# The last up tile and the first two down products in a written engine order, with the down loads issued in written order

## The chip, the cores and the metric

The kernel runs on one core of a Trainium2 chip. The metric is the device time of one execution in microseconds (us). A core has engines that each work through their own list of instructions in order and wait for one another through semaphores: TensorE for matrix products (PE in the profile, PEld its weight loads), VectorE (DVE), ScalarE (ACT), GpSimd (POOL) and SyncE (SP), which here only issues the transfers between device memory and the on-chip buffers.

## The reference

One layer of a streaming encoder on a sequence of 1024 frames with 1024 channels. A token mixer with three attention branches comes first; the change lies behind it, in the channel mixer, whose code is

```python
def _conv_ffn(h, w_up, conv_w, conv_b, w_down):
    a, g = jnp.split(h @ w_up, 2, axis=-1)
    a = lax.conv_general_dilated(a, conv_w[:, None, :], window_strides=(1,),
                                 padding=[(CONV_W - 1, 0)],
                                 dimension_numbers=('NWC', 'WIO', 'NWC'),
                                 feature_group_count=D_FF) + conv_b
    return (jax.nn.gelu(a) * g) @ w_down
...
        h = _rmsnorm(x, norm_g[l, 2]) * (1.0 + sc2) + sh2
        y = _conv_ffn(h, w_up[l], conv_w[l], conv_b[l], w_down[l])
        x = x + g2 * _rmsnorm(y, norm_g[l, 3])
```

`w_up` has 1024 x 5632 elements, `w_down` 2816 x 1024, and the convolution is causal, over three frames, per channel.

## The kernel before

All matrices are float32. Each operand is split into a high part, rounded to the reduced format that TensorE multiplies (ACT makes it, as a copy), and a low part, the difference (DVE makes it); a product is three matmuls: high by high, high by low, low by high. A block product is done by a scheme with seven products of half-size blocks in place of eight, so sums and differences of blocks are formed first on both sides.

**Up.** The 2816 hidden channels are 22 tiles of 128, numbered 0 to 21. `up_tile(f)` does the seven products of tile f (`product`, lines 1246 to 1248, 12 matmuls of 512 columns each). They accumulate in three PSUM banks X, Y and V: X takes the products B11, T2, T3 and T4, Y takes B21, V takes T1 and B22. Between two products on one bank something reads the intermediate sum: `p1` (ACT, line 1263) reads X after B11, `p5` (ACT, line 1269) reads V after T1, `u2` (ACT, line 1272) reads X after T2, and one half of `g` (DVE, line 1278) reads X after T3. The next product on that bank waits for that read. After the seventh product ACT reads the rest of `a` (line 1281). Then come the convolution (ACT line 1285, DVE lines 1286 and 1287), the GELU (ACT line 1288), the product with `g` (POOL line 1289) and `down_left`, which makes the left operands of the down projection from the tiles of a pair, splits them and writes them to device memory (lines 1306 to 1308, `L_spill`; the last two tiles go to `F_spill`). The tiles of those operands rotate over four buffers, so a split waits until the fourth transfer before it has left its buffer.

**Down.** Five chunks of four hidden tiles, and a rest of two. A chunk has seven products of 24 matmuls (lines 1627 to 1629), in `PLAN` order on two sets of four banks, XB and VB; after each, ACT copies or DVE adds the banks into `acc` (lines 1634 and 1632). The left operands are loaded from `L_spill` into `ring`, twelve slots in three buffers (line 1492); these three buffers are those that held the left operands S2, S4 and S3 of the up products, so the first four loads wait until tile 21 is done with S2. The right operands come from four rows of `w_down` per chunk: two tiles `wd` and, for the first chunk, two parts of `work` (line 1507), which takes the place of `big0`, the left operand of B11 and B21. `right_split` (lines 1501 and 1502) splits them, and `total` (line 1537) forms T1 to T4. Four pieces of a small product with `w_ada` (lines 185 to 210) are done beside it.

**Order.** Some stretches are written out by hand: within `tc.manual_schedule(engines=...)` the named engines take the program's order. Everything else is placed by a list scheduler with a timing model, each engine for itself; there the order of the code is only a preference. In the kernel before, tiles 1 to 21 and the whole down part are left to the scheduler, and so is the order of SP's transfers.

Names of a buffer carry a tile or chunk number and a serial number; both are dropped in the profile's names, so `X<-left_S,rT` stands for the products T2 and T3, `V<-left_S,rB` for B22 and `X<-big,rT` for T4.

Of the kernel before, what the change touches and what calls it, by code (L numbers as in the profile page):

```python
# [16 lines left out]
P = 128  # L17
# [4 lines left out]
HALF = 512  # L22
# [38 lines left out]
def encoder_layer(ctx: ExitStack, tc: tile.TileContext, x, w_ada, w_in, w_branch, w_out, w_up, w_down,  # L61
# [1188 lines left out]
    def up_tile(f, r, parts):  # L1250
# [36 lines left out]
        dve.scalar_tensor_tensor(cv[:, 2:], a[:, 0:S - 2], w0[:, f:f + 1], cv[:, 2:], op0=OP.mult, op1=OP.add)  # L1287
        act.activation(cv, cv, AF.Gelu_apprx_tanh)  # L1288
        pool.tensor_tensor(cv, cv, g, op=OP.mult)  # L1289
        down_left(f, cv)  # L1290
# [175 lines left out]
    for f in range(1, NF):  # L1466
        tile_ = up_tile(f, r, [(0, HALF)])
        go(tile_)
        for _ in before:
            pass  # L1470
        if f + 1 < NF:
            r, ws = up_weights(f + 1)
            for _ in ws:
                pass
        go(tile_, 5)
        before = tile_
    for _ in before:
        pass
# [5 lines left out]
    XB = [bank(t, f"X_{i}") for i, t in enumerate("ddss")]  # L1484
    VB = [bank(t, f"V_{i}") for i, t in enumerate("snnn")]
# [11 lines left out]
    def right_split(src, eng, name, alloc=None):  # L1497
        nonlocal n_right
        n_right += 1
        t = alloc(name, (P, 2, HALF)) if alloc else (f4 if n_right % 4 == 0 else k4)(name, F32R, (P, 2, HALF))  # L1500
        act.activation(t[:, 0], src, AF.Copy)  # L1501
        eng.tensor_tensor(t[:, 1], src, t[:, 0].bitcast(F32), op=OP.subtract)
        return t
# [9 lines left out]
    def chunk_load(c):  # L1513
        for k in range(2):
            loaded[c, k] = [w_load(4 * c + 2 * k, raw4),
                             w_load(4 * c + 2 * k + 1, e4 if c else (lambda n: work[:, 6 + k]))]
# [11 lines left out]
    def prepared(c):  # L1528

        src = [{}, {}]  # L1530
        for k in range(2):
            wa, wb = loaded[c, k]
# [67 lines left out]

    chunk_load(0)
    lefts = all_lefts()
    ahead = [next(lefts) for _ in range(L_AHEAD)]
    preps = all_prepared()
    ready = [next(preps) for _ in range(D_AHEAD)]
    G2 = [t2(f"G2_{g}") for g in range(2)]
    G2_AT = {0: (40,), 1: (42, 44), 2: (46,)}
    seen = set()
    for c in range(N_C):
        for n, (banks, starts, into) in enumerate(PLAN):  # L1610
            if n == D_LOAD:
                if c + 1 < N_C:
                    chunk_load(c + 1)
                else:
                    last_in = [w_load(4 * N_C + j, raw4) for j in range(2)]
            nxt_ = next(preps, None)
            if nxt_ is not None:
                ready.append(nxt_)
            nxt_ = next(lefts, None)
            if nxt_ is not None:  # L1620
                ahead.append(nxt_)
            ops = list(zip(ahead.pop(0), ready.pop(0)))
            for i in range(4):
                o = banks[i]
                for k, (l, r) in enumerate(ops):
                    lh, ll = (l[:, j, i * P:(i + 1) * P] for j in range(2))
                    pe.matmul(o, lh, r[:, 0], start=(starts and k == 0), stop=False, skip_group_check=True)  # L1627
                    pe.matmul(o, lh, r[:, 1], start=False, stop=False, skip_group_check=True)  # L1628
                    pe.matmul(o, ll, r[:, 0], start=False, stop=(k == 1), skip_group_check=True)  # L1629
                dst = C[into][i]  # L1630
                if (into, i) in seen:
                    dve.tensor_tensor(dst, dst, o, op=OP.add)  # L1632
                else:
                    act.activation(dst, o, AF.Copy)
                    seen.add((into, i))
# [62 lines left out]
```

## Time and profile before

| | us |
|---|---|
| median of three runs | 1599.38 |
| lowest and highest of them | 1599.19, 1602.44 |
| the profiled execution | 1600.86 |
| its span, first to last instruction | 1599.1 |
| PE busy | 1497.8 (94%) |
| DVE busy | 1187.5 (74%) |
| ACT busy | 786.4 (49%) |
| POOL busy | 561.5 (35%) |

The span is what the trace shows; the device time of that execution is 1.8 us longer. PE's mean granted clock over the span is 0.984 of full speed. The share of busy time is a mean over stages with different limits; the mixer ends and the up part begins at about 925 us, the down part at 1370 us, and the last matmul ends at 1587.2 us. Shares of DMA are of 16 transfer engines.

### The profile page before, as it was taken

The page shows a single profiled execution, that of the slowest core. Times are in us where ns is not written, and L with a number is a line of the kernel's source. Part 1 is how long each engine was busy: PE and PEld are TensorE (multiplying, and loading weights), DVE is VectorE, ACT ScalarE, POOL GpSimd, SP SyncE. Part 2 cuts the span into 40 slices and gives each one's busy share as a digit, 9 for nine tenths or more (in the row PEclk, how much of TensorE's full clock was granted, in tenths as well). Part 3 has the DMA queues.
Part 4 walks back from the last instruction along what each step waited for, and adds up shares of the span by engine and source line. Part 5 has one row for each costly group of instructions (what it writes and reads, how often), then busy time and mean ns, then how long its engine had stood idle before and what let it go on. Part 6 is the DMA issues. An engine that isn't in the chain of part 4 may idle for free.

```text
span 1599.1 us, 21251 instructions
## 1 busy us (share of the span) xinstructions
PE 1497.8 (94%) x7322; PEld 1239.6 (78%) x7322; DVE 1187.5 (74%) x2166; ACT 786.4 (49%) x1462; POOL 561.5 (35%) x408
## 2 busy tenths in 40 slices
PE   3989999989998999989999999999999999899997
PEld 2768888777886888767888787788888887788885
DVE  6765888999669854547536779888777777778768
ACT  4434598786554454542235455555555554522222
POOL 3441544433453543204542223222222221433205
PEclk9999999999998999999999999999999999999999
DMA  9541333423544332346676413544444445996742
GB/s 282 136 106 32 113 110 87 149 80 119 162 143 131 95 117 86 109 145 189 205 273 217 146 53 96 179 164 165 151 150 149 145 146 197 403 350 225 269 174 105
DMA packets 187871, 253.98 MB, mean 159 GB/s; under 512 B 14891, under 2 KB 145139, under 8 KB 187763
## 3 DMA queue, kind: packets, MB, share of 16 engines
q1 hardware_dynamic: 187763, 252.62, 47.4%
q8 instruction: 58, 0.95, 0.2%
q14 instruction: 50, 0.41, 0.1%
HBM read 169.75 MB, written 74.97 MB: 153 GB/s over the span
## 4 chain that ended last, share of the span: by engine, by line
PE 63%; DVE 19%; DMA 6%; ACT 5%; issue 4%; POOL 2%; SPq 1%; DVEq 0%; POOLq 0%; ACTq 0%
PE X L1246 4%; PE X L1247 4%; PE X L1248 4%; PE g L247 4%; PE g L248 4%; PE g L249 4%; DVE ada_acc L198 2%; PE X L1627 2%; PE X L1629 2%; PE X L1628 2%; PE V L1246 2%; PE V L1247 2%; PE V L1248 2%; DVE junk L649 2%; PE V L1629 2%
## 5 line engine op out<-in xcount | busy, mean ns | idle before, releaser
L647 ACT ACTIVATE junk<-sc,thr 128x512 bf16<-128x512 f32 (+2 forms) x93 | 80.2, 862 | 30.7 <-DVE thr L668 25.7
L649 DVE TENSOR_SCALAR_CACHE_REDUCE junk<-sc,thr 128x384 bf16<-128x384 f32 (+2 forms) x93 | 89.6, 964 | 1.8
L1212 POOL TENSOR_TENSOR T<-ua 128x512 f32<-128x512 f32 x21 | 27.2, 1296 | 174.9 <-DVE rT L1198 165.2
L198 DVE SCALAR_TENSOR_TENSOR ada_acc<-ada_raw,c_act,ada_acc 128x256 f32<-128x256 f32 x120 | 81.4, 725 | 1.3 <-DMA ada_raw<-in_w_ada 1.2
L1289 POOL TENSOR_TENSOR cv<-cv,g 128x1024 f32<-128x1024 f32 x22 | 57.6, 2617 | 45.9 <-ACT cv L1288 36.9
L1247 PE MATMUL X<-left_S,rT 128*128 128x512 f32 (+1 forms) x184 | 70.8, 385 | 0.2 <-DVE left_S L1092 0.2
L1246 PE MATMUL X<-left_S,rT 128*128 128x512 f32 (+1 forms) x184 | 70.8, 385 | 0.0
L1248 PE MATMUL X<-left_S,rT 128*128 128x512 f32 (+1 forms) x184 | 70.7, 384 | 0.0
L1632 DVE TENSOR_TENSOR acc<-acc,X 128x512 f32<-128x512 f32 x68 | 45.8, 683 | 16.8 <-PE X L1629 16.5
L1501 ACT ACTIVATE T<-work 128x512 fp32r<-128x512 f32 x40 | 25.2, 631 | 63.7 <-PE V L1629 26.9
L1213 POOL TENSOR_TENSOR ug<-ug 128x512 f32<-128x512 f32 x22 | 32.6, 1482 | 66.5 <-DVE ua L1206 66.5
L1001 POOL TENSOR_TENSOR M<-M,tgb 128x1024 f32<-128x1024 f32 x12 | 30.6, 2559 | 68.1 <-DVE tgb L999 68.1
L1632 DVE TENSOR_TENSOR acc<-acc,V 128x512 f32<-128x512 f32 x56 | 37.8, 683 | 19.2 <-PE V L1629 19.0
L1627 PE MATMUL X<-T,ring 128*128 128x512 f32 x120 | 47.3, 394 | 0.0
L1629 PE MATMUL X<-T,ring 128*128 128x512 f32 x120 | 47.1, 392 | 0.0
L1628 PE MATMUL X<-T,ring 128*128 128x512 f32 x120 | 46.9, 391 | 0.0
L1197 ACT ACTIVATE rT<-ua 128x512 fp32r<-128x512 f32 x45 | 28.2, 627 | 35.9 <-DVE ua L1210 22.9
L1198 DVE TENSOR_TENSOR rT<-ua,rT 128x512 fp32r<-128x512 f32 x45 | 38.9, 865 | 9.3 <-ACT rT L1197 8.8
L1198 DVE TENSOR_TENSOR rB<-ua,rB 128x512 fp32r<-128x512 f32 x44 | 41.2, 939 | 2.0 <-ACT rB L1197 0.9
L1246 PE MATMUL X<-big,rT 128*128 128x512 f32 (+1 forms) x92 | 36.4, 396 | 5.8 <-DVE g L1278 5.8
L1247 PEld LDWEIGHTS X<-left_S,rT 128*128 128x128 f32 x184 | 34.5, 188 | 7.9 <-DVE left_S L1092 0.4
L615 DVE SCALAR_TENSOR_TENSOR sc<-rl,wi,sc 128x512 f32<-128x512 f32 (+3 forms) x30 | 30.2, 1038 | 14.0 <-ACT rl L614 14.0
(982 smaller groups left out, 5563.0 us busy)
## 6 DMA issues: line engine op xcount, KB each, us to landing
ring<-L_spill SPq DMA_DIRECT2D x70, 512.0 KB, 6.1
L_spill<-S SPq DMA_DIRECT2D x40, 512.0 KB, 4.2
L_spill<-A SPq DMA_DIRECT2D x30, 512.0 KB, 3.3
raw_g<-in_w_in SPq DMA_DIRECT2D x24, 512.0 KB, 4.3
ada_raw<-in_w_ada SPq DMA_DIRECT2D x24, 512.0 KB, 3.8
ua<-in_w_up SPq DMA_DIRECT2D x22, 512.0 KB, 4.3
ug<-in_w_up SPq DMA_DIRECT2D x22, 512.0 KB, 3.9
gate_spill<-tg SPq DMA_DIRECT2D x20, 512.0 KB, 2.6
```

The costliest lines, as they stand in the source:

```text
L198: dve.scalar_tensor_tensor(acc[:, k % 2], per_k[k], c_act[:, k:k + 1], acc[:, k % 2], op0=OP.mult, op1=OP.add)
L247: pe.matmul(o, wh[:, k], hh[:, k, ts_], start=(k == 0), stop=False)
L647: act.activation(junk_a[:, 0:n], scores[b], AF.Sign, scale=-1.0, bias=t_f, accum_out=cnt[:, j:j + 1])
L649: dve.tensor_scalar(junk_d[:, 0:n], scores[b], t_f, None, op0=OP.is_lt, op1=OP.add, accum_out=cnt[:, j:j + 1])
L1198: eng.tensor_tensor(hl_[1], src, hl_[0].bitcast(F32), op=OP.subtract)
L1246: pe.matmul(oc, r[:, 0, k], lh, start=(first and k == 0), stop=False, skip_group_check=True)
L1247: pe.matmul(oc, r[:, 0, k], ll, start=False, stop=False, skip_group_check=True)
L1248: pe.matmul(oc, r[:, 1, k], lh, start=False, stop=(last and k == 3), skip_group_check=True)
L1627: pe.matmul(o, lh, r[:, 0], start=(starts and k == 0), stop=False, skip_group_check=True)
L1628: pe.matmul(o, lh, r[:, 1], start=False, stop=False, skip_group_check=True)
L1629: pe.matmul(o, ll, r[:, 0], start=False, stop=(k == 1), skip_group_check=True)
L1632: dve.tensor_tensor(dst, dst, o, op=OP.add)
```

## The change

The last up tile (21), what is left of tile 20, the preparation of the first right operands and the first two down products are put into one written order for ACT, DVE, POOL and PE. In that order tile 21's last product follows the whole first down product, the second down product follows it, and the adds of the first stand between them. The banks are given out anew (three of XB from the tag of Y, three of VB from that of V, one of each from that of X), the fourth split takes a buffer of the larger pool, and of the four pieces of the product with `w_ada` one moves from the first chunk to the second and one from the second to the third. SP's transfers of the down part, up to the fifth product of the last chunk, are issued in the order of the code, and a chunk's four weight loads come at two places of the chunk before it (three at product 2, one at product 4) in place of one.

```diff
@@ -1285,8 +1285,10 @@
         act.activation(cv, a, AF.Identity, bias=cb[:, f:f + 1], scale=w2[:, f:f + 1])
         dve.scalar_tensor_tensor(cv[:, 1:], a[:, 0:S - 1], w1[:, f:f + 1], cv[:, 1:], op0=OP.mult, op1=OP.add)
         dve.scalar_tensor_tensor(cv[:, 2:], a[:, 0:S - 2], w0[:, f:f + 1], cv[:, 2:], op0=OP.mult, op1=OP.add)
+        yield
         act.activation(cv, cv, AF.Gelu_apprx_tanh)
         pool.tensor_tensor(cv, cv, g, op=OP.mult)
+        yield
         down_left(f, cv)
 
 
@@ -1463,26 +1465,23 @@
             pass
 
     before = first
-    for f in range(1, NF):
+    for f in range(1, NF - 1):
         tile_ = up_tile(f, r, [(0, HALF)])
         go(tile_)
         for _ in before:
             pass
-        if f + 1 < NF:
-            r, ws = up_weights(f + 1)
-            for _ in ws:
-                pass
+        r, ws = up_weights(f + 1)
+        for _ in ws:
+            pass
         go(tile_, 5)
         before = tile_
-    for _ in before:
-        pass
 
 
     ring = [opp.tile([P, 4, 2, HALF], F32R, tag="left", name=f"ring{j}") for j in range(3)]
     work = hp.tile([P, NB, S], F32, tag="h", name="work")
     acc = hp.tile([P, NB, S], F32, tag="h", name="acc")
-    XB = [bank(t, f"X_{i}") for i, t in enumerate("ddss")]
-    VB = [bank(t, f"V_{i}") for i, t in enumerate("snnn")]
+    XB = [bank(t, f"X_{i}") for i, t in enumerate("sssd")]
+    VB = [bank(t, f"V_{i}") for i, t in enumerate("nnnd")]
     n_left = 0
 
     def left_load(src):
@@ -1497,7 +1496,7 @@
     def right_split(src, eng, name, alloc=None):
         nonlocal n_right
         n_right += 1
-        t = alloc(name, (P, 2, HALF)) if alloc else (f4 if n_right % 4 == 0 else k4)(name, F32R, (P, 2, HALF))
+        t = alloc(name, (P, 2, HALF)) if alloc else (f4 if n_right % 4 == 0 and n_right > 4 else k4)(name, F32R, (P, 2, HALF))
         act.activation(t[:, 0], src, AF.Copy)
         eng.tensor_tensor(t[:, 1], src, t[:, 0].bitcast(F32), op=OP.subtract)
         return t
@@ -1510,10 +1509,14 @@
     N_C = 5
     loaded = {}
 
-    def chunk_load(c):
-        for k in range(2):
-            loaded[c, k] = [w_load(4 * c + 2 * k, raw4),
-                             w_load(4 * c + 2 * k + 1, e4 if c else (lambda n: work[:, 6 + k]))]
+    def chunk_load(c, which=(0, 1, 2)):
+
+        for j in which:
+            if j == 1:
+                for k in range(2):
+                    loaded[c, 1, k] = w_load(4 * c + 2 * k + 1, e4 if c else (lambda n: work[:, 6 + k]))
+            else:
+                loaded[c, 0, j // 2] = w_load(4 * c + j, raw4)
 
...
+    def down_mm(n, ops):
+        banks, starts, _ = PLAN[n]
+        for i in range(4):
+            o = banks[i]
+            for k, (l, r) in enumerate(ops):
+                lh, ll = (l[:, j, i * P:(i + 1) * P] for j in range(2))
+                pe.matmul(o, lh, r[:, 0], start=(starts and k == 0), stop=False, skip_group_check=True)
+                pe.matmul(o, lh, r[:, 1], start=False, stop=False, skip_group_check=True)
+                pe.matmul(o, ll, r[:, 0], start=False, stop=(k == 1), skip_group_check=True)
+            yield
+
+    seen = set()
+
+    def down_add(n, i):
+        banks, _, into = PLAN[n]
+        dst = C[into][i]
+        if (into, i) in seen:
+            dve.tensor_tensor(dst, dst, banks[i], op=OP.add)
+        else:
+            act.activation(dst, banks[i], AF.Copy)
+            seen.add((into, i))
+
+    def next_ops():
+        nxt_ = next(lefts, None)
+        if nxt_ is not None:
+            ahead.append(nxt_)
+        return list(zip(ahead.pop(0), ready.pop(0)))
+
+    lefts = all_lefts()
+    preps = all_prepared()
+    G2 = [t2(f"G2_{g}") for g in range(2)]
+    G2_AT = {1: (40, 42), 2: (44, 46)}
+
+
     chunk_load(0)
-    lefts = all_lefts()
-    ahead = [next(lefts) for _ in range(L_AHEAD)]
-    preps = all_prepared()
-    ready = [next(preps) for _ in range(D_AHEAD)]
-    G2 = [t2(f"G2_{g}") for g in range(2)]
-    G2_AT = {0: (40,), 1: (42, 44), 2: (46,)}
-    seen = set()
+    with tc.manual_schedule(engines={E.Activation, E.DVE, E.Pool, E.PE}):
+        tile_ = up_tile(NF - 1, r, [(0, HALF)])
+        go(tile_)
+        ready = [next(preps)]
+        go(before)
+        go(tile_)
+        go(before)
+        go(tile_)
+        go(before)
+        ahead = [next(lefts) for _ in range(L_AHEAD)]
+        go(tile_)
+        ready.append(next(preps))
+        for _ in before:
+            pass
+        go(tile_)
+        ready.append(next(preps))
+        go(tile_)
+        for _ in down_mm(0, next_ops()):
+            pass
+        go(tile_)
+        for i in range(4):
+            down_add(0, i)
+        ready.append(next(preps))
+        go(tile_)
+        for i, _ in enumerate(down_mm(1, next_ops())):
+            down_add(1, i)
+        go(tile_)
+    for _ in tile_:
+        pass
+
+    loads = ExitStack()
+    loads.enter_context(tc.manual_schedule(engines={E.SP}))
     for c in range(N_C):
-        for n, (banks, starts, into) in enumerate(PLAN):
...
+        for n in range(len(PLAN)):
+            if c == N_C - 1 and n == 4:
+                loads.close()
+            if c + 1 < N_C:
+                if n == D_LOAD:
+                    chunk_load(c + 1, (0, 1))
+                elif n == 4:
+                    chunk_load(c + 1, (2,))
+            elif n == D_LOAD:
+                last_in = [w_load(4 * N_C + j, raw4) for j in range(2)]
+            if c or n > 1:
+                nxt_ = next(preps, None)
+                if nxt_ is not None:
+                    ready.append(nxt_)
+                for i, _ in enumerate(down_mm(n, next_ops())):
+                    down_add(n, i)
 
             if n == 0:
                 for a in G2_AT.get(c, ()):
```

What moves is shown by the order of instructions on an engine. The first place is ACT around `p_21_0_...<-V`, the read that tile 21's product B22 waits for. `A_19` and `S_19` are splits of `down_left`, `B_0` and `T_0` splits of the first chunk's right operands, `a`, `cv` and `u` belong to tiles 20 and 21. Before:

```order
L1306 ACTIVATE S_19_12132<-S_19_12132 128x512
L1306 ACTIVATE A_19_12144<-cv_12119 128x512
L1501 ACTIVATE B_0_0_12416<-work 128x512
L1197 ACTIVATE rT_21_12158<-T_21_12167 128x512
L1281 ACTIVATE a_12088<-X_12085 128x4x128
L1501 ACTIVATE T_0_0_12425<-work 128x512
L1269 ACTIVATE p_21_0_12249<-V_12245 128x512
L1501 ACTIVATE T_0_1_12429<-work 128x512
```

and now:

```order
L1308 ACTIVATE S_19_12132<-S_19_12132 128x512
L1197 ACTIVATE rT_21_12158<-T_21_12167 128x512
L1281 ACTIVATE a_12088<-X_12085 128x4x128
L1308 ACTIVATE A_19_12144<-cv_12119 128x512
L1285 ACTIVATE cv_12319<-a_12088,ccol 128x1024
L1269 ACTIVATE p_21_0_12272<-V_12268 128x512
L1289 ACTIVATE cv_12319<-cv_12319 128x1024
L1272 ACTIVATE u_21_0_12273<-X_12266 128x512
```

The two splits that read `work`, a buffer filled by a load, stood ahead of the read of V; now none does, and one split that waits for a spill's buffer (`A_19_12144`) still does.

The second place is DVE ahead of `g_...<-X`, the read of tile 21's X that its last product T4 waits for. Before:

```order
L1502 TENSOR_TENSOR T_0_0_12425<-work,T_0_0_12425 128x512
L1502 TENSOR_TENSOR T_0_1_12429<-work,T_0_1_12429 128x512
L1537 TENSOR_TENSOR work<-work 128x512
L1286 SCALAR_TENSOR_TENSOR cv_12277<-a_12088,ccol,cv_12277 128x1023
L196 TENSOR_SCALAR ada_acc<-work,c_act 128x256 x2
L1502 TENSOR_TENSOR T_0_0_12465<-work,T_0_0_12465 128x512
L1275 TENSOR_TENSOR g_12247<-V_12245,u_21_0_12250 128x4x128
L1502 TENSOR_TENSOR B_0_0_12510<-work,B_0_0_12510 128x512
L1287 SCALAR_TENSOR_TENSOR cv_12277<-a_12088,ccol,cv_12277 128x1022
L198 SCALAR_TENSOR_TENSOR ada_acc<-work,c_act,ada_acc 128x256
L1278 TENSOR_TENSOR g_12247<-X_12243,p_21_0_12249 128x4x128
```

and now:

```order
L1540 TENSOR_TENSOR work<-work,wd_12258 128x512
L1501 TENSOR_TENSOR B_0_0_12359<-work,B_0_0_12359 128x512
L1540 TENSOR_TENSOR work<-work,wd_12262 128x512
L1501 TENSOR_TENSOR B_0_1_12362<-work,B_0_1_12362 128x512
L1309 TENSOR_TENSOR uf_20_12365<-cv_12319,uf_20_12365 128x512
L1309 TENSOR_TENSOR uf_20_12369<-cv_12319,uf_20_12369 128x512
L1275 TENSOR_TENSOR g_12270<-V_12268,u_21_0_12273 128x4x128
L1540 TENSOR_TENSOR work<-wd_12258 128x512
L1501 TENSOR_TENSOR T_0_0_12387<-work,T_0_0_12387 128x512
L1540 TENSOR_TENSOR work<-wd_12262 128x512
L1501 TENSOR_TENSOR T_0_1_12391<-work,T_0_1_12391 128x512
L1278 TENSOR_TENSOR g_12270<-X_12266,p_21_0_12272 128x4x128
```

The two convolution steps of tile 20 (lines 1286 and 1287) stand ahead of this stretch now, the steps of the product with `w_ada` are gone from it, and the totals and splits for the second and third down products are in it.

The third place is SP's list from tile 19's first spill to the first loads of `ring`. Before:

```order
L1308 DMA L_spill<-S_19_12125 128x1024
L1507 DMA work<-in_w_down 128x1024 x2
L1308 DMA L_spill<-A_19_12140 128x1024
L185 DMA work<-in_w_ada 128x4x256 x2
L1308 DMA L_spill<-S_19_12127 128x1024
L1308 DMA L_spill<-S_19_12132 128x1024
L1308 DMA L_spill<-A_19_12144 128x1024
L1507 DMA wd_12506<-in_w_down 128x1024
L1492 DMA ring_12383<-L_spill 128x1024 x4
```

and now:

```order
L1310 DMA L_spill<-S_19_12125 128x1024
L1506 DMA wd_12505<-in_w_down 128x1024
L1310 DMA L_spill<-A_19_12140 128x1024
L1310 DMA L_spill<-S_19_12127 128x1024
L1310 DMA L_spill<-S_19_12132 128x1024
L1506 DMA work<-in_w_down 128x1024 x2
L1310 DMA L_spill<-A_19_12144 128x1024
L1491 DMA ring_12243<-L_spill 128x1024 x4
```

The loads for the product with `w_ada` and one load of a later chunk's weights no longer stand ahead of the first ring loads.

## Rows read from the trace of the kernel before

**Rows 1.** Busy time by stretch: each engine, then PE's granted clock, DMA share, GB/s.

```profile
1350.00:1353.00 3.00, 0.48 (x3) 0.04 (x1) 2.47 (x5) 2.54 (x6) 0.00 (x0) 0.93 1.03 392
1353.00:1357.00 4.00, 3.85 (x11) 3.10 (x12) 4.00 (x8) 2.76 (x5) 0.83 (x1) 0.63 1.06 416
1365.00:1370.00 5.00, 4.92 (x12) 3.93 (x13) 5.00 (x8) 1.33 (x3) 3.13 (x2) 0.54 1.03 415
1370.00:1586.80 216.80, 216.80 (x960) 178.45 (x959) 164.44 (x265) 64.39 (x115) 67.92 (x53) 1.00 0.69 253
```

**Rows 2.** PE in order of time: start, length, what, [idle before, ended by].

```profile
1338.88 0.40 PE L1248 MATMUL X<-left_S,rT 128*128 128x512 f32 x1
...
1350.09 0.40 PE L1248 MATMUL X<-left_S,rT 128*128 128x512 f32 x1
1353.15 0.79 PE L1246 MATMUL V<-left_S,rB 128*128 128x512 f32 x1 [2.67 <-ACT p L1269]
...
1357.33 0.39 PE L1246 MATMUL X<-left_S,rT 128*128 128x512 f32 x1
...
1359.89 0.40 PE L1248 MATMUL X<-left_S,rT 128*128 128x512 f32 x1
1365.08 0.80 PE L1246 MATMUL X<-big,rT 128*128 128x512 f32 x1 [4.79 <-DVE g L1278]
...
1370.04 0.40 PE L1627 MATMUL X<-B,ring 128*128 128x512 f32 x1
```

**Rows 3.** ACT in order of time, from tile 19's convolution on.

```profile
1329.77 1.25 ACT L1285 ACTIVATE cv<-a,ccol 128x1024 f32<-128x1024 f32 x1
...
1334.93 0.63 ACT L1501 ACTIVATE B<-wd 128x512 fp32r<-128x512 f32 x1 [2.40 <-DMA wd<-in_w_down]
1335.47 1.04 ACT L1288 ACTIVATE cv<-cv 128x1024 f32<-128x1024 f32 x1
...
1347.45 0.63 ACT L1306 ACTIVATE A<-cv 128x512 fp32r<-128x512 f32 x1 [4.06 <-DMA L_spill<-S]
1350.46 0.63 ACT L1501 ACTIVATE B<-work 128x512 fp32r<-128x512 f32 x1 [2.38 <-DMA work<-in_w_down]
```

**Rows 4.** DVE in order of time, the same stretch.

```profile
1333.18 1.28 DVE L1287 SCALAR_TENSOR_TENSOR cv<-a,ccol,cv 128x1022 f32<-128x1022 f32 x1
...
1352.34 0.69 DVE L1537 TENSOR_TENSOR work<-work 128x512 f32<-128x512 f32 x1
1352.95 0.69 DVE L1198 TENSOR_TENSOR rT<-T,rT 128x512 fp32r<-128x512 f32 x1
...
1357.16 2.33 DVE L1286 SCALAR_TENSOR_TENSOR cv<-a,ccol,cv 128x1023 f32<-128x1023 f32 x1
...
1364.34 0.68 DVE L1278 TENSOR_TENSOR g<-X,p 128x512 f32<-128x512 f32 x1
```

**Rows 5.** POOL in order of time: tile 19's product with g.

```profile
1336.59 2.40 POOL L1289 TENSOR_TENSOR cv<-cv,g 128x1024 f32<-128x1024 f32 x1 [5.24 <-ACT cv L1288]
```

**Rows 6.** PE in order of time: two short waits early in the up part.

```profile
925.45 0.39 PE L1246 MATMUL X<-big,rB 128*128 128x256 f32 x1 [1.95 <-DVE xn L1071]
...
976.55 0.50 PE L1246 MATMUL X<-big,rT 128*128 128x512 f32 x1 [0.54 <-DVE g L1278]
```

**Rows 7.** Busy time by stretch, right behind these two waits.

```profile
976.50:979.00 2.50, 2.44 (x11) 2.01 (x12) 2.50 (x6) 0.69 (x2) 0.00 (x0) 1.00 0.35 106
925.40:928.00 2.60, 2.55 (x13) 2.55 (x14) 1.91 (x4) 0.57 (x2) 1.07 (x2) 0.60 0.84 231
```

**Rows 8.** The chain that ended last, in order of time: two loads, start and length.

```profile
1331.38 3.47 DMA wd<-in_w_down
...
1343.59 6.85 DMA work<-in_w_down
```

**Rows 9.** The ring buffers' loads from 1345 to 1380 us.

```profile
DMA to landing us min/median/max: 9.9/10.2/10.6
```

More of the change, by code (lines that the diff above doesn't have):

```diff
@@ L1531, in prepared @@
         for k in range(2):
-            wa, wb = loaded[c, k]
+            wa, wb = loaded[c, 0, k], loaded[c, 1, k]
             src[k].update(B11=wa[:, 0:HALF], B12=wa[:, HALF:], B21=wb[:, 0:HALF], B22=wb[:, HALF:])
@@ L1599, in final_block @@
             nc.sync.dma_start(out[tb * P:(tb + 1) * P, es], xr[:, es])
-    chunk_load(0)
-    lefts = all_lefts()
-    ahead = [next(lefts) for _ in range(L_AHEAD)]
-    preps = all_prepared()
-    ready = [next(preps) for _ in range(D_AHEAD)]
-    G2 = [t2(f"G2_{g}") for g in range(2)]
-    G2_AT = {0: (40,), 1: (42, 44), 2: (46,)}
-    seen = set()
-    for c in range(N_C):
-        for n, (banks, starts, into) in enumerate(PLAN):
[L1611 to L1635, printed above, removed]
```

## The prediction

> **What bounds the kernel now.** I read the page's time slices first: PE is at nine tenths or more in nearly all, and the only weak one behind the mixer, ahead of the last, is that from 1359 to 1399 us, where tile 21's last up products meet the first down product. Next I read busy time by stretch. From 1370.0 to 1586.8 us PE is busy for the whole 216.8 us at full clock while DMA is at 0.69, so nothing is to be had there but matmuls; from 1350 to 1370 us PE is idle or its granted clock is down, 0.54 to 0.63 for some us [rows 1]. These are stretches at 1.2 GHz within a run at 2.4.
>
> PE's list in order of time shows what happens. Between the last matmul of tile 21's product T2 at 1350.09 us and the first down matmul at 1370.04 us there are 36 matmuls (B22, T3, T4), so 37 steps in 19.95 us. At full clock a step is (1359.89 - 1357.33) / 11 = 0.233 us, and 37 steps are 8.6 us. **The seam therefore loses 11.3 us**, in four parts [rows 2]:
> - 2.8 us from 1350.09 to 1353.15, waiting for ACT's read `p` of V;
> - 1.4 us in the 12 matmuls behind it (4.18 in place of 2.80 us), at the lower clock;
> - 5.0 us from 1359.89 to 1365.08, waiting for DVE's read `g` of X;
> - 2.2 us in the 12 matmuls behind that.
>
> ACT's and DVE's lists say why the reads were late. ACT's `p` of V stood behind a split that waited 4.06 us for a spill buffer and a split of `work` that waited 2.38 us for a load [rows 3]; both waits were in ACT's queue, not for V. Tile 19's GELU had already been held 2.40 us by a split of `wd` ahead of it [rows 3]. On DVE `g` of X came at 1364.34 us, though X was complete at 1360.29 us [rows 2, 4]; the steps between are splits of down operands, convolution steps and the product with `w_ada`.
>
> **The change part by part.** I follow the new order of each engine with the durations of before.
>
> *T4 of tile 20* comes earlier, right behind tile 20's T3 and two matmuls of tile 21. T3's last matmul stood at 1338.88 us with 0.40 us [rows 2]; one matmul fewer is ahead of it, so it ends at 1339.05. T4 could start at 1339.35, but needs DVE's `g` of tile 20: 0.68 us, and 0.06 us from its end to PE (1365.02 to 1365.08) [rows 2, 4], so 1339.85. That is a new pause of 0.5 us, and the first matmul behind such a pause took 0.50 for 0.39 us [rows 6]: +0.6 us. DVE is free by then: with the two `wd` splits gone from ahead of the GELU, tile 19's second convolution step ends 0.8 us earlier, at 1333.6, GELU (1.04) and POOL's product (2.40) end at 1337.1 [rows 3 to 5], and two sums at a step of 0.6 us [rows 4] at 1338.3.
>
> *PE from there* has 72 matmuls up to the end of tile 21's T3 (T4 of tile 20, then B21, T1, T2, B22 and T3), 16.8 us: T1 is complete at 1348.5, T2 at 1351.3, the first down product is due at 1356.7.
>
> *The wait for `p` goes.* What still stands ahead of it on ACT is the split of `A_19`, which waits for the buffer of the first spill of tile 19. That spill leaves at about 1340.4. How long it takes in the new traffic is not in the trace; the nearest rows are a lone load, 3.47 us, and one behind several others, 6.85 us [rows 8]. So the buffer is free at 1343.9 to 1347.3, `A_19` (0.63) and the convolution's first step (1.25) end by 1349.2 [rows 3], `p` by 1349.8, and B22 is due at 1351.1. Late next: nothing; 1.3 us are left at worst, and I cost it at 0. What hides it is T2; without that cover it costs up to 3.3 us (a landing of 10.2 us [rows 9], 1.9 us of wait and 1.4 of restart).
>
> *The wait for `g` of X goes behind the first down product*, 24 matmuls of about 0.23 us or 5.5 us, which now stands between T3 and T4. T4 is due at 1362.5. DVE has 12 steps from the first total over `work` to `g` (the order above), at 0.6 us 7.2 us, with two hand-overs to ACT of 0.63 us. The two `work` loads leave when Y is complete, at 1345.7, land at 1349.2 to 1352.6, the second 1.3 us later (0.52 MB at 416 GB/s [rows 1]). `g` ends at 1358.6 to 1361.1; one convolution step drawn out from 1.28 to 2.33 us, as one was [rows 4], makes it 1362.2. I cost it at 0; it is the closest cover of all.
>
> *The first ring loads* can leave only when T2 is done with the buffer, at 1351.3, whatever SP's order. The bounds are again 3.47 and 6.85 us, with the second load 1.3 us behind the first: first 1354.8 to 1358.2, second 1356.1 to 1359.4. They are due at 1356.7 and, three matmuls later, 1357.4. So the wait is 0 to 2.0 us. In the old seam, with a median of 10.2 us [rows 9], `w_ada` loads, three spills and a weight load stood right ahead of the ring's (the order above); now two `work` loads and one spill do, so I take the middle, 5.2 us: **+0.3 us**.
>
> The Trainium skill has a price for this, in "DMA: Bandwidth & Descriptors", section "Anatomy of one DMA": a fixed cost of about 2.0 us plus the bytes at 436 GB/s, fitted for transfers from GpSimd. For 0.52 MB that is an estimate of 3.2 us; the lone load agrees nearly (3.47 us), the queued ones do not (6.85 and 10.2 us). By the page the pair would be in time and the sum 0.3 us lower.
>
> *The rest.* The new banks are read well before they are needed: `a` of Y21 on DVE at about 1347, X of tile 20 on ACT at 1344. The second down product needs the splits of B21 (done by 1356) and follows T4 without a wait. Behind the seam PE was never idle [rows 1], and the moved pieces of `w_ada` and the written loads only have to stay ahead of it. They start a chunk of 7 x 5.5 = 38.5 us with its loads issued four to five products, 22 to 27 us, before, against 10.2 us of landing in the worst stretch seen [rows 9]. Cost 0.
>
> **The sum**: -11.3 + 0.6 + 0.3 = -10.4 us. The profiled execution has a span of 1599.1 us and took 1600.86 us; by this it becomes 1588.7 and 1590.5. That execution is 1.5 us above the median of the three runs, 1599.38 us; from the median, **1589.0 us**.
>
> **The rivals.**
> - *The ring pair is late* (chance 0.06). For it speaks that DMA is at 1.03 to 1.06 and every ring load of the old seam took 9.9 to 10.6 us [rows 1, 9]; against it that four `w_ada` and weight loads are gone from ahead. At 10.2 us the pair lands at 1361.5 and 1362.8: a wait of 5.4 us and a restart of 2.2 us, a gain of 11.3 - 0.6 - 7.6 = 3.1 us: 1596.3 us.
> - *DVE is late for `g`* (0.15). If the `work` loads take 10.2 us, the second lands at 1357.2, and ten steps and two hand-overs later it is 1364.5: a wait of 2.1 us and a restart of 1.4 us, 1592.5 us.
> - *The clock falls after short pauses* (0.08). Behind a wait of 1.95 us the granted clock was 0.60, behind one of 0.54 us it stayed at 1.00 [rows 6, 7]. Should it fall at both new pauses, each costs a restart of 1.4 to 2.2 us: about 3.6 us, 1592.6 us.
>
>   The Trainium skill speaks for this one, "TensorE: Matmul & The Clock Gate", section "A second HAM failure mode: psum-queue depth-cycling": a kernel that cycles through PSUM banks and pauses briefly but often had its clock go back and forth. This trace doesn't bear it out at 0.54 us.
> - *Nothing is gained* (0.04): the seam is bound by the transfers and the pauses only change places, 1599 us. Against it: both reads waited in a queue, with V and X complete.
> - *Slower* (0.04): SP's written order. A load that waits for its buffer now holds back all behind it, the weights of the next chunk among them, which before went out wherever the scheduler had placed them. If PE waits at the start of each of the four later chunks as it did at the old seam, 4.8 us and a restart of 2.2 us each, that is 28 us: 1617 us. It decides from 10.4 / 4 = 2.6 us per chunk. Against it stand the 22 to 27 us of lead.
>
> **How the numbers follow.** The forecast has the remaining chance, 0.63, with a range of its own from 1588.1 (neither new pause) to 1590.8 us (the ring wait at its bound of 2.0 us). About 0.2%, 3.2 us, is what a measurement of this kernel can tell from no change. Faster by more: the forecast, DVE late, the clock and half of the ring's case, 0.89. Within: nothing gained and the other half, 0.07. Slower: 0.04. The range for 8 in 10 runs from 1587.3 (0.8 us below the forecast's own low end, for the end of the program, where I count nothing) to 1593.5 us, so that it holds the cases of DVE and the clock.
>
> **What would show it.** In the changed trace: PE's list from T2 of tile 21 to the second down product with no wait over 2 us, a pause of about 0.5 us before tile 20's T4, granted clock 1.00 from 1340 to 1370 us; ACT's `p` of V within 1 us of V's last matmul; DVE's `g` of tile 21 ended before the first down product; the last matmul at about 1576.4 us. A wait for a ring load over 2 us, a wait at T4 of tile 21, or PE idle at the start of a later chunk would show the matching step wrong; the forecast as a whole fails if the time is above 1593.5 us.

## The result: 1590.1 us, and the profile after

Over six runs each the changed kernel took 1590.1 us (median; 1588.2 to 1596.3) and the kernel before 1600.7 us (1598.1 to 1603.4): a ratio of 0.9938, 95% interval 0.9917 to 0.9958, or 9.9 us less, between 6.7 and 13.3. In a later set of runs (e7) the ratio was 0.9955 (0.9939 to 0.9972).

PE's waits from 1320 us to the end, in the changed kernel (total us, times, longest):

```profile
engine line waited for: us in total, times, longest us
PE X L1246 <- DVE g L1278: 0.3, 1, 0.3
PE X L1610 <- DMA ring<-L_spill: 0.3, 1, 0.3
```

The waits for `p` and for `g` of tile 21 [rows 2] are gone, and two short ones are new. PE alone by stretch (busy time, granted clock, DMA share, GB/s), to be read against [rows 1]:

```profile
1338.00:1341.00 3.00, 2.68 (x12) 1.00 0.25 101
1350.00:1356.00 6.00, 6.00 (x27) 1.00 0.99 393
1356.00:1360.00 4.00, 3.69 (x17) 1.00 1.02 418
1360.00:1366.00 6.00, 6.00 (x28) 1.00 1.03 414
1370.00:1576.00 206.00, 206.00 (x913) 1.00 0.71 261
```

The clock stays at its upper level, 1.00, all through, though the DMA engines are as full as they were. PE's list at the places of the two pauses, at T4 of tile 21, and at the program's last matmul:

```profile
1338.17 0.40 PE L1248 MATMUL X<-big,rB 128*128 128x512 f32 x1
1338.89 0.50 PE L1246 MATMUL X<-big,rT 128*128 128x512 f32 x1 [0.32 <-DVE g L1278]
...
1355.59 0.44 PE L1610 MATMUL X<-B,ring 128*128 128x512 f32 x1
...
1356.09 0.39 PE L1612 MATMUL X<-B,ring 128*128 128x512 f32 x1
1356.79 0.50 PE L1610 MATMUL X<-B,ring 128*128 128x512 f32 x1 [0.31 <-DMA ring<-L_spill]
...
1361.71 0.40 PE L1246 MATMUL X<-big,rT 128*128 128x512 f32 x1
...
1575.73 0.40 PE L1592 MATMUL X<-wl,ring 128*128 128x512 f32 x1
```

Steps are 0.23 us, so the pause before tile 20's T4 costs 0.72 - 0.23 + 0.11 (the longer first matmul) = 0.60 us, and that at the second ring load 0.70 - 0.23 + 0.11 = 0.58 us. ACT and DVE, answering to [rows 3, 4]:

```profile
1342.96 0.62 ACT L1308 ACTIVATE A<-cv 128x512 fp32r<-128x512 f32 x1
...
1347.39 0.60 ACT L1269 ACTIVATE p<-V 128x512 f32<-128x512 f32 x1 [2.67 <-PE V L1248]
...
1351.44 0.63 ACT L1500 ACTIVATE B<-work 128x512 fp32r<-128x512 f32 x1 [0.66 <-DMA work<-in_w_down]
```

```profile
1351.44 0.78 DVE L1540 TENSOR_TENSOR work<-work,wd 128x512 f32<-128x512 f32 x1 [3.47 <-DMA work<-in_w_down]
...
1360.09 0.68 DVE L1278 TENSOR_TENSOR g<-X,p 128x512 f32<-128x512 f32 x1
```

`p` now waits for V itself, ahead of the split that waits for the load; `A_19` waits for nothing; `g` ends at 1360.77 us, 0.94 us before T4. SP's queue shows what leaves in the seam (issue time, how long the issuing took, number of loads):

```profile
1344.66 1.87 SPq L1506 DMA_DIRECT2D work<-in_w_down  x2
1346.63 0.72 SPq L1310 DMA_DIRECT2D L_spill<-A  x1
1350.18 4.54 SPq L1491 DMA_DIRECT2D ring<-L_spill  x8
```

The first `work` load landed 6.8 us after its issue, the second 7.6 us, the first ring load about 5.3 us.

Single executions of one kernel differ by several us, mostly ahead of the seam. So beside the ratios I use **the seam's own length in the trace**: from the first matmul of tile 20's B22 to the last matmul of the program. It is 1586.81 - 1331.22 = 255.59 us before and 1575.73 - 1330.06 = 245.67 us after, 9.92 us less. In the kernel before, and in e6 and e9, one matmul of tile 21 stands ahead of this stretch, so that it holds 1079 matmuls there and 1080 in all others: beside the others these three seams count 0.23 us more.

| kernel | ratio to before (95%) | seam, us |
|---|---|---|
| before | 1 | 255.59 |
| changed; again, in a later set (e7) | 0.9938 (0.9917-0.9958); 0.9955 (0.9939-0.9972) | 245.67; 246.39 |
| e1 no cover | 0.9980 (0.9969-0.9992) | 253.32 |
| e2 splits ahead of `p` | 0.9993 (0.9982-1.0003) | 252.62 |
| e3 no written load order | 1.0003 (0.9991-1.0015) | 255.84 |
| e5 old `w_ada` table | 0.9973 (0.9957-0.9989) | 249.94 |
| e6 before + load order + table | 0.9937 (0.9916-0.9959) | 244.97 |
| e9 before + load order alone | 0.9924 (0.9907-0.9941) | 244.90 |
| e4 no short pauses; again | 0.9947 (0.9929-0.9964); 0.9937 (0.9913-0.9961) | 244.51; 244.52 |

### The profile page after: what moved, and what is told of

It reads as the page before. It is cut to its first block, busy times and chain, and to the rows that moved or that the text cites. A ratio compares the mean times of both kernels' runs of the same rounds, so it can differ in the third digit from the quotient of the medians.

```text
span 1588.0 us, 21237 instructions
## 1 busy us (share of the span) xinstructions
PE 1495.3 (94%) x7322; PEld 1236.2 (78%) x7322; DVE 1179.6 (74%) x2166; ACT 786.0 (49%) x1462; POOL 564.0 (36%) x408
## 3 DMA queue, kind: packets, MB, share of 16 engines
q1 hardware_dynamic: 187763, 252.62, 47.8%
## 4 chain that ended last, share of the span: by engine, by line
PE 69%; DVE 17%; issue 4%; ACT 4%; DMA 3%; POOL 1%; SPq 1%; DVEq 0%; POOLq 0%; ACTq 0%
PE X L1246 4%; PE X L1247 4%; PE X L1248 4%; PE g L247 4%; PE g L248 4%; PE g L249 4%; PE X L1610 2%; PE X L1611 2%; PE X L1612 2%; DVE junk L649 2%; PE V L1246 2%; PE V L1247 2%; PE V L1248 2%; DVE ada_acc L198 2%; PE V L1610 2%
## 5 line engine op out<-in xcount | busy, mean ns | idle before, releaser
L1621 DVE TENSOR_TENSOR acc<-acc,X 128x512 f32<-128x512 f32 x68 | 45.8, 682 | 13.7 <-PE X L1612 13.3
L1247 PEld LDWEIGHTS X<-left_S,rT 128*128 128x128 f32 x184 | 34.5, 187 | 8.0 <-DVE left_S L1092 0.4
L1248 PEld LDWEIGHTS X<-left_S,rT 128*128 128x128 f32 x184 | 34.4, 187 | 7.7
```

The source lines that it names most:

```text
L1247: pe.matmul(oc, r[:, 0, k], ll, start=False, stop=False, skip_group_check=True)
L1248: pe.matmul(oc, r[:, 1, k], lh, start=False, stop=(last and k == 3), skip_group_check=True)
L1621: dve.tensor_tensor(dst, dst, banks[i], op=OP.add)
```

## The experiments

**e1: the cover taken away.**

```diff
         go(tile_)
-        for _ in down_mm(0, next_ops()):
-            pass
         go(tile_)
+        for _ in down_mm(0, next_ops()):
+            pass
```

> The changed kernel with one edit: tile 21's T4 stands on PE ahead of the first down product again, no matmuls between T3 and T4. Theory (the down product only serves as cover for DVE's read g of X): g ends at about 1360.8 us as it does now, T4 is due at 1355.6 us, so a wait of about 5.2 us before T4, about 2.2 us of restart at the lower clock behind it as behind the 5.0 us wait of the old seam, and the 0.6 us wait for the second ring load goes, its time covered by T4: +6.8 us against the changed kernel's 1590.1 us, 1596.9 us. Rival (the order of ACT and DVE alone made the gain, the cover is not needed): no wait over 1 us at T4, 1590 us. Second rival (the wait is there but the clock is not lost behind it): +4.6 us, 1594.7 us.

PE's list of e1 at T4:

```profile
1362.31 0.80 PE L1246 MATMUL X<-big,rT 128*128 128x512 f32 x1 [5.70 <-DVE g L1278]
1362.90 0.63 PE L1247 MATMUL X<-big,rT 128*128 128x512 f32 x1
```

The wait is back, 5.70 us, and so is the lower clock (0.63 us for a matmul of 0.39). The seam is 7.65 us longer than in the changed kernel (expected 6.8; 0.5 us of it is a short pause further on), the ratio 0.0042 higher, 6.7 us. Within the changed kernel the down product is needed as cover.

**e2: two splits ahead of `p` on ACT.**

```diff
         go(before)
+        ready.append(next(preps))
         go(tile_)
         go(before)
         ahead = [next(lefts) for _ in range(L_AHEAD)]
         go(tile_)
-        ready.append(next(preps))
```

> The changed kernel with one edit: on ACT and DVE the two splits of work (B21 of the first chunk) stand ahead of the read p of V again. Theory (p was late because it stood in ACT's queue behind splits that wait for a load): the second work load lands at about 1353.0 us, p ends at about 1354.1 us, tile 21's product B22 is due at 1350.1 us, so a wait of about 4.0 us at B22, 1.4 to 2.2 us of restart behind it, and the ring wait of 0.6 us goes: +5.2 us, 1595.3 us; no wait at T4, since the down product is still its cover. Rival (p was late for another reason, the full spill buffer or the loads' own lateness in the old order): no wait at B22, 1590 us.

ACT's list of e2, then PE's at B22:

```profile
1358.35 0.63 ACT L1500 ACTIVATE B<-work 128x512 fp32r<-128x512 f32 x1 [8.55 <-DMA work<-in_w_down]
...
1360.25 0.58 ACT L1269 ACTIVATE p<-V 128x512 f32<-128x512 f32 x1
```

```profile
1360.89 0.80 PE L1246 MATMUL V<-left_S,rB 128*128 128x512 f32 x1 [5.65 <-ACT p L1269]
```

PE waited 5.65 us at B22 and the seam was 6.95 us longer; expected 4.0 and 5.2. The first `work` load took 8.0 us here instead of 6.8. So both reasons of the prediction hold as far as e1 and e2 go: undo either place in the written order and its wait is back.

**e3: the written load order taken away.** Only the `manual_schedule` for SP goes; ACT, DVE, POOL and PE keep their written block.

```diff
-    loads = ExitStack()
-    loads.enter_context(tc.manual_schedule(engines={E.SP}))
...
-            if c == N_C - 1 and n == 4:
-                loads.close()
```

> The changed kernel without the written order of the down loads on SP; everything else as changed. Theory (behind the seam PE never waited, so the written loads only have to stay ahead of it, cost and gain 0): 1590 us within 0.2%, PE busy for the whole stretch from 1370 to 1576 us. Rival (the loads' order carries part of the gain): PE waits for ring or weight loads at the start of chunks, 1593 us or more. Rival on the other side (the written order holds weight loads back and costs something): 1587 us or less.

Theory and measurement part here: the whole gain is lost. SP's queue and PE's waits of e3:

```profile
1349.37 1.12 SPq L185 DMA_DIRECT2D work<-in_w_ada  x2
1352.64 8.58 SPq L1491 DMA_DIRECT2D ring<-L_spill  x8
```

```profile
1362.21 0.79 PE L1610 MATMUL X<-B,ring 128*128 128x512 f32 x1 [4.00 <-DMA ring<-L_spill]
...
1398.82 0.79 PE L1610 MATMUL X<-T,ring 128*128 128x512 f32 x1 [2.09 <-DVE acc L1621]
```

Without the written load order the scheduler puts a `w_ada` pair ahead of the first ring loads here too, though the table is moved, and the first ring load lands 9.5 us after its issue, not 5.3. The sum closes: 4.16 us of late start at 1362 and 2.75 of restart, 2.24 at 1398 and 1.61 of restart, less the 0.58 us pause of the changed kernel, is 10.2 us; the seam is 10.17 us longer. So the written engine order, with the moved table but without the load order, gains nothing: ratio 1.0003 (0.9991 to 1.0015).

**e5: the old `w_ada` table under the written load order.**

```diff
-    G2_AT = {1: (40, 42), 2: (44, 46)}
+    G2_AT = {0: (40,), 1: (42, 44), 2: (46,)}
```

> The changed kernel with the old table of w_ada pieces, {0: (40,), 1: (42, 44), 2: (46,)}: the written order of the down loads stays, but one w_ada pair (two loads of 0.52 MB) is issued ahead of the first ring loads again and its eight DVE steps stand among those ahead of g. Theory (the experiment without the written load order lost 10 us because its two w_ada loads stood right ahead of the first ring pair, which then came 4.0 us late): the ring pair is about 4 us late again, 2.2 us of restart behind it, less the 0.6 us wait of now, and no wait at T4, since the down product that covers it is itself late: +5.6 us over the changed kernel, a ratio of about 0.9973 to the kernel before. Rival (it was the order of the other loads, the weight and ring loads behind the first eight): no wait over 1 us at the first down product, ratio 0.994.

SP's queue of e5, then PE at its first ring load:

```profile
1349.92 1.90 SPq L185 DMA_DIRECT2D work<-in_w_ada  x2
1351.87 1.43 SPq L1506 DMA_DIRECT2D wd<-in_w_down  x1
1353.68 7.55 SPq L1491 DMA_DIRECT2D ring<-L_spill  x8
```

```profile
1362.22 0.61 PE L1610 MATMUL X<-B,ring 128*128 128x512 f32 x1 [2.97 <-DMA ring<-L_spill]
```

A `w_ada` pair stands ahead of the ring loads again, and a `wd` load that the changed kernel issues before the `work` loads. The first ring load is issued 20.1 us behind the seam's first matmul in the changed kernel, in e3 and in e5 alike; PE starts on it at 25.5, 29.7 and 28.7 us. PE waited 2.97 us in e5 and the seam was 4.27 us longer, the ratio 0.0035 higher; expected 4 and 5.6. Beside the changed kernel of the same set of runs (e7) the seam was only 3.55 us longer and the ratio 0.0018 higher, with intervals that overlap, so the cost is clear in the trace and not in the time. Issued at the same moment, the ring loads land later by what stands ahead of them in the queue. The old table costs 5.9 us less than no written order does; 3.9 us of that is the second wait with its restart, which is missing in e5.

**e6 and e9: the load order alone.** Both start from the kernel before, where the scheduler places up tiles, splits and matmuls. e9 adds only these lines; e6 has the moved table too.

```diff
+    loads = ExitStack()
+    loads.enter_context(tc.manual_schedule(engines={E.SP}))
     for c in range(N_C):
         for n, (banks, starts, into) in enumerate(PLAN):
+            if c == N_C - 1 and n == 4:
+                loads.close()
```

> The kernel before with two parts of the change alone: the moved table of w_ada pieces and the written order of the down loads on SP; up tiles, banks, ACT, DVE and PE as the scheduler places them. With the w_ada loads gone from the seam the scheduler itself puts 18 matmuls of the first down products between T3 and T4 of tile 21, but on ACT a split of work still stands ahead of the read p of V. Theory (three limits that are late at nearly the same time: p behind a load on ACT, g without cover, ring loads behind w_ada; each one left costs its own wait): the wait for p stays with its restart, about 4.2 us, the wait for g goes for the most part behind 4.2 us of matmuls; -5 to -7 us, ratio 0.9956 to 0.9969. Rival (one limit that is left gives everything away, since all three end at the same loads): ratio 0.999 to 1.0. Second rival (the written load order is the whole of the gain): ratio 0.994.

> The kernel before with one part of the change alone: the written order of the down loads on SP; the old table of w_ada pieces stays. The first w_ada pair then stands behind ten ring loads, and the work loads have no other load between them and the spills of tile 19. Theory (what counts is which loads stand ahead of the work and ring loads in the seam; the written order sets that, the table needs not be moved, and ACT's, DVE's and PE's order follows from it): ratio 0.994 to the kernel before, no PE wait over 1 us from 1320 us to the end. Rival (the table is needed too, as the experiment with the old table in the changed kernel suggests, which lost 0.2 to 0.3% by it): a wait of 3 us or more at the first down product or at T4, ratio 0.997 or above.

Both gain all of it, so the moved table isn't needed here. The code says why e5 differs. In the kernel before, the stretch that the written load order covers begins with a pair of ring loads (the fifth), and the `w_ada` pair comes behind it, so behind ten ring loads; in the changed kernel six pairs of ring loads stand in the block ahead of that stretch, which with the old table begins with the `w_ada` pair, and nothing orders that behind the ring loads. And e6's theory of three limits, each with its own price, falls with its number: 10.6 us of seam instead of 5 to 7. The lines of e9, SP's queue, then ACT, DVE and PE:

```profile
1344.27 0.32 SPq L1308 DMA_DIRECT2D L_spill<-S  x1
1344.68 1.87 SPq L1507 DMA_DIRECT2D work<-in_w_down  x2
...
1352.67 7.40 SPq L1492 DMA_DIRECT2D ring<-L_spill  x10
1361.03 1.67 SPq L185 DMA_DIRECT2D work<-in_w_ada  x2
```

```profile
1347.72 0.63 ACT L1306 ACTIVATE A<-cv 128x512 fp32r<-128x512 f32 x1 [2.21 <-DMA L_spill<-S]
1350.41 0.63 ACT L1501 ACTIVATE B<-work 128x512 fp32r<-128x512 f32 x1 [2.05 <-DMA work<-in_w_down]
...
1352.47 0.58 ACT L1269 ACTIVATE p<-V 128x512 f32<-128x512 f32 x1
```

```profile
1361.30 0.68 DVE L1278 TENSOR_TENSOR g<-X,p 128x512 f32<-128x512 f32 x1
```

```profile
1353.11 0.50 PE L1246 MATMUL V<-left_S,rB 128*128 128x512 f32 x1 [0.46 <-ACT p L1269]
...
1358.81 0.39 PE L1631 MATMUL X<-B,ring 128*128 128x512 f32 x1
...
1362.94 0.40 PE L1246 MATMUL X<-big,rT 128*128 128x512 f32 x1
```

On ACT `p` still stands behind the splits of `A_19` and of `work`, as before [rows 3], but what they wait for comes sooner: 2.21 us for the spill instead of 4.06, 2.05 for the load instead of 2.38. `p` starts 19.1 us behind the seam's first matmul instead of 21.3, and PE waits 0.46 us instead of 2.67. `g` starts at 27.9 us instead of 33.1, with no `w_ada` step ahead of it, and the scheduler, with the ring loads early in its plan, itself puts 18 down matmuls (1358.81 to 1362.94) ahead of T4. They cover `g`, which ends at 1361.98 us; without them T4 would have waited about 3.2 us by these rows. The `w_ada` pair leaves behind ten ring loads and PE waits for nothing else. So e9 is one edit but more than one cause: the loads come sooner, and the scheduler, planning with them, also makes the cover that e1 shows to be needed.

**e4, and e8 beside e7: the two short pauses.** T3 of tile 20 goes into the block ahead of tile 21's first product, and the first down product takes the first operand pair through all four banks before the second.

```diff
-        go(tile_, 5)
+        go(tile_, 5 if f < NF - 2 else 4)
...
+        go(before)
         go(tile_)
         ready = [next(preps)]
...
+        for h in range(2 if pairs else 1):
...
+                    if pairs and k != h:
+                        continue
```

> The changed kernel with two edits against the two short pauses that are left: tile 20's T3 is written into the block ahead of tile 21's first product, so that 12 matmuls instead of 2 stand between T3 and T4 of tile 20; and the first down product runs its 12 matmuls of the first operand pair on all four banks before those of the second, so that the second ring load is needed 12 matmuls after the first and not 3. Theory (these two pauses of 0.6 us each are all that is left of the seam): both go, no PE wait from 1330 us to the end, -1.1 to -1.2 us, 1588.9 us. Rival (a pause comes back at tile 21's T4, which is now due 1.2 us earlier, while DVE's g of X had 0.94 us to spare and keeps its time): a wait of up to 0.3 us at T4, -0.8 us. Rival (the pauses cost nothing because something behind them waits anyway): 1590.1 us.

> The changed kernel itself, unedited, on the same chip as the version without the two short pauses, so that the two can be compared beside each other. All theories: ratio 0.994 to the kernel before.

> The version without the two short pauses (as in the earlier run of it), on the same chip as the changed kernel. Theory: its seam is 1.16 us shorter in the trace (from the first matmul of tile 20's B22 to the last matmul of the program 244.51 us against 245.67 us), so it is 1.2 us or 0.07% faster than the changed kernel, ratio 0.993; by less than the intervals can tell. Rival (something behind the seam takes the 1.2 us back): the same ratio as the changed kernel, or above it.

In e4 and e8 PE waits for nothing from 1320 us to the end, and the seam is 244.5 us, 1.16 us shorter, as expected. In time it can't be told from the changed kernel: 0.9937 (0.9913 to 0.9961) beside 0.9955 (0.9939 to 0.9972). Of the kernels tried, e4's seam is the shortest and e9 has the lowest ratio, but the intervals of e4, e6, e9 and the changed kernel overlap.

**e10 to e12: how much `g` has to spare, and what a wait does to the clock.** A line of DVE is done four, six or nine times over. Each was run once, so only the traces are read.

```diff
+            for _ in range(4 if f == NF - 1 else 1):
                 dve.tensor_tensor(view(g, 1), ps(X), ps(p5), op=OP.add)
```

> The changed kernel with DVE's read g of X in tile 21 done four times over instead of once (each time the same sum into the same place), so that it ends 1.8 us later. Theory (g had 0.94 us to spare behind the first down product): a wait of 0.3 to 0.9 us at tile 21's T4, the granted clock stays at 1.00 behind it, as behind the pauses of 0.5 us. Rival (the cover has more to spare than the trace shows): no wait. Second rival (any wait drops the clock): 1.4 us or more of slower matmuls behind it.

> The same with the read done six times, 3.0 us later. Theory: a wait of 1.5 to 2.1 us at T4, and, as behind the wait of 1.95 us in the kernel before, a lower granted clock behind it, about 1.4 us of restart. Rival (the clock falls only behind waits of 2.7 us and more, or by what stood ahead of the wait): granted clock 1.00 behind it.

> The same with the read done nine times, 4.8 us later. Theory: a wait of 3.3 to 3.9 us at T4 and 1.4 to 2.2 us of restart behind it, as behind the waits of 2.7 and 5.0 us of the kernel before. Rival (the restart grows with the wait): between the two others in proportion.

DVE's repeated line in e10, and PE at T4 in e10, e11 and e12, each from the list of its own kernel:

```profile
1362.46 2.86 DVE L1279 TENSOR_TENSOR g<-X,p 128x512 f32<-128x512 f32 x4
```

```profile
1365.37 0.50 PE L1246 MATMUL X<-big,rT 128*128 128x512 f32 x1 [1.11 <-DVE g L1279]
1365.71 0.40 PE L1247 MATMUL X<-big,rT 128*128 128x512 f32 x1
```

```profile
1355.68 0.50 PE L1611 MATMUL X<-B,ring 128*128 128x512 f32 x1 [1.56 <-DMA ring<-L_spill]
...
1364.61 0.79 PE L1246 MATMUL X<-big,rT 128*128 128x512 f32 x1 [2.56 <-DVE g L1279]
1365.19 0.63 PE L1247 MATMUL X<-big,rT 128*128 128x512 f32 x1
```

```profile
1366.81 0.80 PE L1246 MATMUL X<-big,rT 128*128 128x512 f32 x1 [4.73 <-DVE g L1279]
1367.41 0.63 PE L1247 MATMUL X<-big,rT 128*128 128x512 f32 x1
```

The waits are 1.11, 2.56 and 4.73 us, above what was expected (0.3 to 0.9, 1.5 to 2.1, 3.3 to 3.9), because a repetition took 0.72 us and not the 0.6 that was reckoned: three, five and eight of them are 2.2, 3.6 and 5.8 us. What `g` has to spare hardly changed. In e10 and e11 it started 31.1 and 31.8 us behind the seam's first matmul, in the changed kernel 30.0, but the ring loads and with them T4 were late by nearly as much: the first end of `g` lay 0.95 to 0.97 us before T4 was due in all three, 0.94 in the changed kernel and 1.00 in e7. The clock held behind 1.11 us, and behind 1.56 us at e11's ring load (granted clock 1.00 in the 1.2 us after it); it fell to 0.50 behind 2.56 and 4.73 us, and to 0.60 on the mean of 2.6 us behind 1.95 us before [rows 7]. Up to the first step of 0.23 us again, the restarts behind T4's waits cost 0.1, 1.7 and 2.5 us, the last above the expected 1.4 to 2.2. They don't simply grow with the wait: behind 4.00 us (e3) it was 2.75, behind 5.65 and 5.70 us (e2, e1) 1.5 and 1.8. In e11 and e12 PE waits once more, 1.58 and 1.49 us for DVE's sums some 30 us later, and the clock stays at 1.00 there.

## Why the prediction was right, and where its reasons were not

The forecast was 1589.0 us (1587.3 to 1593.5) and a gain of 10.4 us; measured were 1590.1 us and 9.9 us (6.7 to 13.3).

- **The seam's 11.3 us**: right. The seam got shorter by 9.92 us, holds one matmul more (0.23 us), and still has 1.18 us of pauses: 11.3 us. e4, with no wait left, is 11.1 us shorter than before and also has that matmul more: 11.3 us.
- **Tile 20's T4, +0.6 us**: measured 0.60.
- **The wait for `p`, at 0**: right; `A_19` had its buffer in time. That the place in ACT's queue decides is shown by e2 for the loads as they land in the changed kernel; e9 shows that the same place costs 0.46 us when they land sooner.
- **The wait for `g`, at 0, "the closest cover of all"**: right, by 0.94 us, with the first `work` load landing at the upper bound (6.8 us, the bound was 6.85). Where the loads came later still (e10, e11), the ring loads behind them came later too, and T4 with them; the prediction reckoned the two apart. e1 and e10 show the price of less cover.
- **The ring pair, +0.3 us within 0 to 2.0**: mis-sized, 0.58 us. That this run came so near is luck: by the same reckoning the pair cost 1.10, 1.31, 1.70 and 2.41 us in the four other runs of the same loads (e12, e7, e10, e11), the last above the bound, its first ring load landing after 7.1 us. And the sentence that the loads can leave "only when T2 is done with the buffer, whatever SP's order" took the order to be without effect because it does not move the issue. It moves the landing: 9.5 us behind a `w_ada` pair (e3), 5.3 without.
- **"The rest. Cost 0"**: this step failed. "The moved pieces of `w_ada` and the written loads only have to stay ahead of it" is true of what lies behind the seam, where PE was busy for all 206 us, but the written loads are what the gain hangs on. The number came out all the same because the ring's term had already been reckoned without the `w_ada` pair; the reason for that, SP's order, was counted elsewhere at nothing. In the rival "the ring pair is late" the same thing stood with a price, 7.6 us of wait and restart; e3 measured 6.9 us there.
- **The gain put down to the order on PE, ACT and DVE**: not shown. That order alone gains nothing (e3), the load order as the only edit all (e9). Inside the changed kernel, where the engines' order is fixed by hand, each place is needed (e1, e2). Left to itself the scheduler finds an order as good once the loads are out of the way, cover included.
- **Rivals**: the clock didn't fall behind the short pauses; SP's written order held nothing back that PE needed; DVE was in time.

The Trainium skill has the rule for the queue in "DMA: Bandwidth & Descriptors", section "Queues, rings and completion order": on each DMA engine the descriptors of a queue are taken in the order of its ring. The traces agree: the ring loads come later by what was issued just ahead of them, 9.5 us in e3 against 5.3.

What stays open: how much of the old seam's loss lay in the `w_ada` pair and how much in the two `wd` loads (three in e9) that the written order also takes out of it. e5 puts the pair and one `wd` load ahead of the ring and costs 4.3 us of 10; no run separated them in the kernel before. Nor did a run put the written load order under the old engine order as it stood: in e6 and e9 the scheduler placed the engines anew, so how much its new order adds to the earlier loads is not shown.

## What to carry to other kernels

A wait's last link is not its cause: here two engines' reads were late in their own queues, and both stood behind the same crowded stretch of transfers, so four added lines that order the loads gave what the whole change gives, and the rewritten block of four engines without them nothing. Before an order is written by hand on the engines, ask what stands ahead in the load queue of each transfer that the stage waits for, and move what isn't needed yet behind it. A part counted at nothing should be undone alone, as e3 does: it may carry the whole sum.

## What the runs showed of the hardware

In e3's later wait DVE's steps were drawn out while POOL ran its totals back to back. DVE, then POOL, of e3:

```profile
1396.42 1.75 DVE L1501 TENSOR_TENSOR T<-work,T 128x512 fp32r<-128x512 f32 x1
1398.09 1.87 DVE L1621 TENSOR_TENSOR acc<-acc,X 128x512 f32<-128x512 f32 x3
1399.89 0.68 DVE L1501 TENSOR_TENSOR B<-wd,B 128x512 fp32r<-128x512 f32 x1
```

```profile
1395.91 1.72 POOL L1540 TENSOR_TENSOR work<-wd,wd 128x512 f32<-128x512 f32 x1
1397.58 1.72 POOL L1540 TENSOR_TENSOR work<-wd,work 128x512 f32<-128x512 f32 x1
```

A split took 1.75 us, the time of one POOL step beside it, and 0.68 us once POOL was done (at 1399.3 us); the sums from PSUM between them took 0.62 us each, also beside POOL. The Trainium skill says in "SBUF — State Buffer", section "SBUF: two separate sides", that a DVE step with two SBUF inputs and a GpSimd step that reads SBUF exclude each other for a whole instruction. That is what these rows look like, though no run here took POOL's steps away.
